# Which weight pairs are summed ahead, when, and a reciprocal on 128x256

## The chip, the cores and the metric

The kernel runs on one core of a Trainium2 chip. The metric is the device time of one execution in microseconds (us), as the median of several runs. The core has a matmul engine (PE; its weight loads are shown apart as PEld), a vector engine (DVE), a scalar engine (ACT), GpSimd (POOL), and SyncE (SP), whose queue issues nearly all transfers (DMAs) between the chip's memory and the on-chip buffers.

## The reference

A decoder trunk of two layers over 512 tokens with 1024 features, in float32. The part of each layer that matters here:

```python
h = rmsnorm(x, g_mix)
z = h @ w_in        # split into attention q, k, v; retention q, k, v, g; two gates
ya = sliding_window_sink_attention(aq, ak, av, sinks) @ w_a
r = chunkwise_retention(rq, rk, rv)
r = r * lax.rsqrt(jnp.mean(r * r, axis=-1, keepdims=True) + EPS)
yb = (r.reshape(B, S, RET_V) * jax.nn.silu(rg)) @ w_b
x = x + (jax.nn.sigmoid(ga) * ya + jax.nn.sigmoid(gb) * yb) @ w_out
h2 = rmsnorm(x, g_mlp)
x = x + jnp.square(jax.nn.relu(h2 @ w_up)) @ w_down
```

`w_in` is 1024 x 5888 here (46 units of 128 columns), `w_b` and `w_out` are 1024 x 1024, `w_up` is 1024 x 4096 and `w_down` 4096 x 1024. A last RMS norm follows the two layers.

## The kernel before

**Layout.** Features lie on the 128 partitions and the 512 tokens in the columns; x is eight chunks of 128x512. Weights are streamed in units of 128x1024 in an order fixed when the program is written (`unit_order`).

**Two parts for each number.** Every operand of a matmul is split into a high part, rounded to the type that PE multiplies fast, and a low part, the rest. A product is three matmuls: high by high, high by low, low by high (`products`, L332 to L334). For a weight unit, ACT copies `hi` (L286) and DVE subtracts to get `lo` (L287). `split_until` does this three units ahead of their use; `hi`, `lo` and the raw weights have three buffers each.

**Pairs.** Most chunks of `w_b` (the first four), `w_out` (the last six) and `w_up` (all but the first four) are computed two at a time by a scheme with seven products in place of eight: x or its counterpart is cut into blocks, sums of these blocks ("forms", `sum_input`, L590 to L594) are multiplied by sums of the two chunks' weights. A pair takes four parts (units), of which the last is half as wide. A narrow pair (`narrow_pair`) multiplies 256 columns at a time with `products`; a wide one (`wide_pair`, chunks 6 to 31 of `w_up`) has its high by high and high by low products in one matmul of 512 columns (L1321), and the low by high in one of 256 (L1322).

**Where the weight sums come from.** Usually DVE makes them in four adds of 128x512 just before the parts are split (`add_part`, L252, L255, L259, L260). Such a pair loads half of its first chunk w1 and its second chunk w2 into two of the three raw buffers, and the other half of w1 into a buffer of the larger pool `big` (seven buffers of 128x1024); part 2 takes one more of these. The sums of the five pairs in `PARKED` are made ahead instead, in every layer: `raws_ahead` loads both chunks into two `big` buffers (L234), `sums_ahead` makes four adds (L241 to L244) and writes the four results to the chip's memory (L246, "parking"), and `load_part` fetches them later (L219): seven loads for the pair in place of three, and no add at that time. Before the change these are the first two pairs of `w_b` and all three of `w_out`.

**Where the sums ahead are placed.** `ahead()` makes the oldest loaded sum and then loads the next pair; two loads precede the first. Its five calls stand, before the change, behind the second head's retention keys and queries (`qk(1)`), behind units 1 and 3 of the retention values (`values`), and behind units 1 and 3 of `w_a`. The last call in `values` stands ahead of the evacuation of the four value banks (`split`, ACT L342 and DVE L343).

**The stages of a layer, in order**, for layer 0: attention's projections, the gates and the first half of the retention projections with attention as a background task that is advanced between matmuls (to about 145 us); the values, and `w_a` (to about 192 us); the rest of `w_in` with retention in the background; `w_b` (about 320 to 360 us); `w_out` (two plain chunks, then three narrow pairs, to about 402 us); the MLP, which begins with a group of four plain chunks of `w_up` in four units, then pairs 4 (narrow) and 6 (wide) back to back, then `w_down` chunks and `w_up` pairs by turns.

**The MLP's norm.** Sums of squares of x come from PE as a matmul with ones, so that every partition holds all tokens' sums (L461). `inverse_rms` takes a root on ACT (L462) and a reciprocal on DVE (L463), both on 128x512; `Rms.finish` calls it behind the second unit of the first group of `w_up`. The four banks of that group are evacuated with it (`put_up`, L1298), and those of pair 4 (`positive`, L1287). The norm ahead of the projections is `folded`: its sums of squares lie on half of the partitions; both norms use the same function.

**Order.** Each engine and SP work strictly in order. That order is made when the program is built: a planner goes through the instructions in the order in which they are written, with estimated durations, and lets a later one go first where an earlier one isn't ready by its estimate. `tc.issue_after(ins)` keeps what stands in it behind `ins`. Buffers are given out by the same planner when their last reader is done.

Of the kernel before, what the change touches and what calls it, by code (L numbers as in the profile page):

```python
# [13 lines left out]
AF = mybir.ActivationFunctionType  # L14
# [4 lines left out]
P = 128  # L19
T = 512  # L20
D = 1024
# [29 lines left out]
ASIDE = 48  # L51
FIRST_WIDE, LAST_WIDE = 6, 32
BETWEEN = (0, 2, 4, 5)
PARKED = (("w_b", 0), ("w_b", 2), ("w_out", 2), ("w_out", 4), ("w_out", 6))
H = T // 2
CROSSED = (0, 1, 4, 5, 2, 3, 6, 7)

# [65 lines left out]
def view(slot):  # L123
    return slot[0][:, slot[1], :]
# [3 lines left out]
def decoder(ctx, tc, xT, x_first, w_in, w_a, w_b, w_out, w_up, w_down, tables, decay, band, triangles, g_last, out):  # L128
    nc = tc.nc
# [8 lines left out]
    ps_aux = ctx.enter_context(tc.tile_pool(name="ps_aux", bufs=3, space=PSUM))  # L138
# [4 lines left out]
    def temp(name="t"):  # L143
        return tmp.tile([P, T], F32, tag="t", name=name)

    def big(name, dtype=F32):
        return tmp.tile([P, 2, T], dtype, tag="big", name=name, bufs=7)

    def bank(pool, name):
        return pool.tile([P, T], F32, tag=pool.name, name=name)  # L150
# [8 lines left out]
    eps, half, keep = (little_x[:, a : a + n] for a, n in ((0, 1), (8, N_KV), (16, P // 2)))  # L159
# [45 lines left out]

    park = {at: dram.tile([P, 4, T], F32, name="park_%s_%d" % at) for at in PARKED}

# [22 lines left out]
    def raws_ahead(layer, src, j):  # L230

        two = [big("ahead").rearrange("p a t -> p (a t)") for _ in range(2)]
        for b, w in enumerate(two):
            nc.sync.dma_start(w, weights[src][layer, j + b])  # L234
        return two
# [56 lines left out]
    def unit(name, layer):  # L292
        i = state["next"]
        assert order[i][:2] == (layer, name), (order[i], layer, name)
        state["next"] += 1
        split_until(i + 3)
        return parts.pop(i)
# [7 lines left out]
    ones = const.tile([P, P], F32R, name="ones")  # L305
# [20 lines left out]
    def products(ps, pairs, start, stop, resume=False):  # L326


        n = len(pairs)
        for i, ((ah, al), (bh, bl)) in enumerate(pairs):  # L330
            more = {"skip_group_check": True} if resume else {}
            nc.tensor.matmul(ps, ah, bh, start=start and i == 0, stop=False, **more)  # L332
            nc.tensor.matmul(ps, ah, bl, start=False, stop=False, **more)  # L333
            nc.tensor.matmul(ps, al, bh, start=False, stop=stop and i == n - 1, **more)  # L334

    def split(hi, lo, src, scale=None):

        if scale is None:
            nc.scalar.activation(hi, src, AF.Copy)  # L339
            nc.vector.tensor_tensor(lo, src, f32(hi), ALU.subtract)  # L340
        else:
            nc.scalar.activation(hi, src, AF.Copy, scale=scale)  # L342
            nc.vector.scalar_tensor_tensor(lo, src, scale, f32(hi), ALU.mult, ALU.subtract)  # L343
# [15 lines left out]
    def advance(rate=1.0):  # L359

        credit[0] += rate
        while credit[0] >= 1.0:
            credit[0] -= 1.0
            while background:
                try:
                    next(background[0])
                    break
                except StopIteration:
                    background.pop(0)

    def drain():
        while background:
            advance()

    def chunk(name, layer, moving, evacuate, rate=1.0):

        hi, lo = unit(name, layer)
        n = len(moving)
        ps = bank(ps_mm, "mm")
        pairs = [((hi[:, k * P : (k + 1) * P], lo[:, k * P : (k + 1) * P]), moving[k]) for k in range(n)]  # L380
        advance(rate)
        products(ps, pairs[: n // 2], True, False)
        advance(rate)
        products(ps, pairs[n // 2 :], False, True)
        evacuate(ps)
# [57 lines left out]
    def inverse_rms_apart(both, n, dest):  # L443
# [10 lines left out]
        nc.sync.dma_start(row, own[0 : P : P // NB, :])  # L454
        nc.sync.dma_start(dest, row.rearrange("b t -> (b t)").unsqueeze(0).broadcast_to([P, T]))

    def inverse_rms(both, n, dest):

        ps = bank(ps_aux, "ssq")
        for i, part in enumerate(both):  # L460
            nc.tensor.matmul(ps, ones, part, start=i == 0, stop=i == len(both) - 1)  # L461
        nc.scalar.activation(dest, ps, AF.Sqrt, bias=eps, scale=1.0 / n)  # L462
        nc.vector.reciprocal(dest, dest)  # L463
# [12 lines left out]
    class Rms:  # L476
# [7 lines left out]

        def finish(self):
            self.value = tmp.tile([P, T], F32, tag="rstd", name="rstd", bufs=2)
            inverse_rms(self.parts, D, self.value)


    def end(layer, uT):  # L490
# [76 lines left out]
    def layer_body(layer):  # L567
# [3 lines left out]
        def rstd():  # L571
            return rms_mix.value
# [78 lines left out]
        def scaled_tables(i):  # L651
            raw, t = big("rawtab"), big("tab")
            nc.sync.dma_start(raw, tables[:, 2 * i : 2 * i + 2, :])
            nc.vector.tensor_tensor(t, raw, rstd().unsqueeze(1).broadcast_to([P, 2, T]), ALU.mult)
            return [t[:, j, :] for j in range(2)]
# [253 lines left out]
        def put_ret(box, h):  # L909
            def put(ps):  # L910
                if not ret_tabs:
                    ret_tabs.extend(scaled_tables(1))
                hi, lo = slots.one(), slots.one()
                split(view(hi), view(lo), rotate(ps, ret_tabs))
                box[h] = (hi, lo)

            return put

        def qk(h, rate=1.0):
            chunk("w_in", layer, xs, put_ret(rk, h), rate)  # L920
            chunk("w_in", layer, xs, put_ret(rq, h), rate)

        rv = {}

        def values(pair, between=lambda: None):

            banks = [bank(ps_mm, "rv") for _ in range(NB)]
            for u in range(4):
                hi, lo = unit("w_in", layer)
                for j in range(2):  # L930
                    k = 2 * u + j
                    cols = slice(j * T, (j + 1) * T)
                    for b, ps in enumerate(banks):
                        at = slice(b * P, (b + 1) * P)
                        products(
                            ps, [(tuple(m[:, at] for m in xs[k]), (hi[:, cols], lo[:, cols]))], k == 0, k == KD - 1
                        )
                    advance()
                if u % 2:
                    between()  # L940
            for b, ps in enumerate(banks):
                hi, lo = slots.one(), slots.one()
                split(view(hi), view(lo), ps, rcol[:, b : b + 1])
                rv[pair, b] = (hi, lo)
# [3 lines left out]
        def put_rg(i):  # L948
            def put(ps):
                if i % 2 == 0:  # L950
                    two = rg_tiles[i // 2] = big("z")
                    rg[i], rg_next[i + 1] = two[:, 0, :], two[:, 1, :]
                else:
                    rg[i] = rg_next.pop(i)
                nc.vector.tensor_tensor(rg[i], ps, rstd(), ALU.mult)
                if i >= 4:
                    silu(i)

            return put

        def silu(i):
            s = temp("sig")
            nc.scalar.activation(s, rg[i], AF.Sigmoid)
            nc.vector.tensor_tensor(rg[i], rg[i], s, ALU.mult)
# [129 lines left out]
        qk(0, PACE)  # L1094
        for i in range(4):
            chunk("w_in", layer, xs, put_rg(i), PACE)
        drain()
        rstd_columns()
        with tc.issue_after(last_exp[0]):
            for hs in (slice(0, T // 2), slice(T // 2, T)):  # L1100
                nc.scalar.activation(x[:, :, hs], x[:, :, hs], AF.Sigmoid)
            for i in range(4):
                silu(i)
        to_load, to_sum = [(layer, *at) for at in PARKED], []

        def load_ahead():
            if to_load:
                to_sum.append((*to_load[0][1:], raws_ahead(*to_load.pop(0))))

        def ahead():  # L1110
            if to_sum:
                with tc.issue_after(last_low[0]):
                    sums_ahead(*to_sum.pop(0))
            load_ahead()

        load_ahead()
        load_ahead()
        qk(1)
        ahead()
        values(0, ahead)  # L1120


        aT = [(a_h[:, c, :], a_l[:, c, :]) for c in range(4)]
        for u in range(4):
            hi, lo = unit("w_a", layer)
            for j in range(2):
                c = 2 * u + j
                ps = bank(ps_mm, "mm")
                pairs = []
                for k in range(4):  # L1130
                    cols = slice(k * 256 + j * P, k * 256 + (j + 1) * P)
                    pairs.append(((hi[:, cols], lo[:, cols]), aT[k]))
                products(ps, pairs, True, True)
                nc.vector.tensor_tensor(mixed[c], mixed[c], ps, ALU.mult)
            if u % 2:
                ahead()
        for t in a_t:
            slots.give(*t[1])
# [2 lines left out]
        qk(2)  # L1141
        qk(3)
        values(1)
        drain()
        background.append(retention(1))
# [301 lines left out]
    for layer in range(DEPTH):  # L1447
        layer_body(layer)
# [175 lines left out]
```

## Time and profile before

| what | value |
|---|---|
| median of three runs | 1478.03 us (1477.93 to 1478.52) |
| the profiled execution's own time | 1478.12 us |
| its span (first to last instruction) | 1476.3 us |
| PE busy | 1465.4 us, 99% |
| PE weight loads busy | 1249.4 us, 85% |
| DVE busy | 1169.0 us, 79% |
| ACT busy | 809.3 us, 55% |
| DMA | 194.45 MB, 132 GB/s on average |

A row of the instructions in order of time reads: start in us from the span's start, length, engine, line, operation, output<-inputs, sizes, count; in brackets the engine's idle time before it and what ended it. A row of the list of waits reads: engine and line, what it waited for, us in total, times, the longest. A group in the profile of one line gives shortest, median and longest duration in ns and the first and last start. In the list of transfers stand line, count, KB each and the median us from issue to landing. Matmuls are pipelined and their ends are modelled, so a busy PE may still lose time between starts.

### The profile page before, as it was taken

Reading aid. Unit: us, or ns where it says so; the run is one execution under the profiler, and the core shown is the slowest. Engines: PE = TensorE matmul, PEld = TensorE weight load, DVE = VectorE, ACT = ScalarE, POOL = GpSimd, SP = SyncE. Lnnn points to the kernel's source line nnn. Section 1 sums busy time; section 2 is a strip of 40 time slices with the busy share of each in tenths; the row PEclk is TensorE's granted clock in tenths of the full one; section 3 lists DMA queues with packets and bytes.
Section 4 is the critical chain, followed back from the end, with each engine's and each line's share of the span. In section 5 each row is a group of like instructions: output and inputs, shape, how many; then the busy total and the mean of one; then the engine's idle time right before and its main releaser. Section 6 shows DMA issues by size and latency. Waiting matters only on the chain.

```text
span 1476.3 us, 20212 instructions
## 1 busy us (share of the span) xinstructions
PE 1465.4 (99%) x7466; PEld 1249.4 (85%) x7466; DVE 1169.0 (79%) x1920; ACT 809.3 (55%) x1296; POOL 3.8 (0%) x14
## 2 busy tenths in 40 slices
PE   9999999999999999999999999999999999999998
PEld 7888788888988888888888888888989888888887
DVE  7998778778898787776678987786888977878763
ACT  6656356654674445444455753656547654444553
POOL 0000000000000000000000000000000000000000
PEclk9999999999999999999999999999999999999999
DMA  6423943356523332333443258333655223333241
GB/s 226 134 88 94 316 134 96 105 170 223 165 79 115 100 111 89 107 107 115 164 124 98 86 167 289 104 103 104 205 180 168 96 93 98 114 101 113 89 140 57
DMA packets 71042, 194.45 MB, mean 132 GB/s; under 512 B 8456, under 2 KB 8608, under 8 KB 70944
## 3 DMA queue, kind: packets, MB, share of 16 engines
q1 hardware_dynamic: 70656, 192.65, 40.6%
q8 instruction: 58, 0.95, 0.3%
q10 hardware_dynamic: 288, 0.52, 0.1%
q14 instruction: 40, 0.33, 0.1%
HBM read 171.63 MB, written 18.89 MB: 129 GB/s over the span
## 4 chain that ended last, share of the span: by engine, by line
PE 90%; issue 5%; DVE 3%; DMA 1%; ACT 1%; POOLq 0%; SPq 0%; DVEq 0%; ACTq 0%
PE mm L334 22%; PE mm L332 22%; PE mm L333 22%; PE mm L1321 10%; PE mm L1322 5%; PE rv L332 2%; PE rv L334 2%; PE rv L333 2%; DVE lo L287 1%; PE score L828 1%; PE r L332 1%; PE r L334 1%; PE r L333 1%; DMA park_w_b<-ahead 0%; PE pT L783 0%
## 5 line engine op out<-in xcount | busy, mean ns | idle before, releaser
L333 PE MATMUL mm<-r,hi 128*128 128x512 f32 (+1 forms) x1568 | 572.8, 367 | 0.0
L332 PE MATMUL mm<-r,hi 128*128 128x512 f32 (+1 forms) x1568 | 570.4, 367 | 1.2 <-DVE r L343 1.2
L334 PE MATMUL mm<-r,lo 128*128 128x512 f32 (+1 forms) x1568 | 564.2, 367 | 0.4
L286 ACT ACTIVATE hi<-raw 128x1024 fp32r<-128x1024 f32 (+1 forms) x334 | 334.1, 1002 | 394.7 <-PE mm L333 193.9
L287 DVE TENSOR_TENSOR lo<-raw,hi 128x512 fp32r<-128x512 f32 (+1 forms) x335 | 384.1, 1150 | 113.1 <-ACT hi L286 109.7
L332 PEld LDWEIGHTS mm<-r,hi 128*128 128x128 f32 x1568 | 294.1, 188 | 48.4 <-DVE r L343 1.5
L334 PEld LDWEIGHTS mm<-r,lo 128*128 128x128 f32 x1568 | 293.7, 188 | 48.9 <-DVE lo L287 1.6
L333 PEld LDWEIGHTS mm<-r,hi 128*128 128x128 f32 x1568 | 294.5, 188 | 45.9
L1321 PE MATMUL mm<-r,hi 128*128 128x512 f32 x728 | 251.9, 391 | 0.0
L1322 PE MATMUL mm<-r,lo 128*128 128x256 f32 x728 | 200.3, 277 | 2.9 <-DVE lo L287 2.7
L1321 PEld LDWEIGHTS mm<-r,hi 128*128 128x128 f32 x728 | 136.4, 188 | 28.3
L1322 PEld LDWEIGHTS mm<-r,lo 128*128 128x128 f32 x728 | 136.7, 188 | 7.0 <-DVE lo L287 4.5
L1401 DVE TENSOR_TENSOR x<-x,mm 128x512 f32<-128x512 f32 x56 | 37.7, 686 | 29.3 <-PE mm L334 29.3
L1394 ACT ACTIVATE z<-z 128x512 f32<-128x512 f32 x56 | 32.5, 624 | 48.3 <-DVE z L1374 48.3
L333 PE MATMUL rv<-lo,r 128*128 128x512 f32 x128 | 49.8, 389 | 0.0
L334 PE MATMUL rv<-hi,r 128*128 128x512 f32 x128 | 49.5, 389 | 0.0
L332 PE MATMUL rv<-hi,r 128*128 128x512 f32 x128 | 49.5, 390 | 0.0
L340 DVE TENSOR_TENSOR r<-z,r 128x512 fp32r<-128x512 f32 x64 | 42.8, 684 | 2.8 <-ACT r L339 2.6
L339 ACT ACTIVATE r<-z 128x512 fp32r<-128x512 f32 x64 | 38.5, 620 | 7.9 <-DVE z L1055 7.9
L855 ACT ACTIVATE sm<-sm,st 128x256 f32<-128x256 f32 (+1 forms) x64 | 30.2, 473 | 19.2 <-DVE st L843 18.9
L1374 DVE SCALAR_TENSOR_TENSOR z<-z,rstd 128x512 f32<-128x512 f32 x52 | 35.7, 686 | 0.6
L343 DVE SCALAR_TENSOR_TENSOR r<-x,r 128x512 fp32r<-128x512 f32 x32 | 23.9, 745 | 7.6 <-ACT r L342 7.5
(267 smaller groups left out, 1696.2 us busy)
## 6 DMA issues: line engine op xcount, KB each, us to landing
raw<-w_in_in SPq DMA_DIRECT2D x89, 512.0 KB, 3.7
raw<-w_down_in SPq DMA_DIRECT2D x64, 512.0 KB, 3.6
raw<-w_up_in SPq DMA_DIRECT2D x36, 512.0 KB, 3.6
raw<-w_up_in SPq DMA_DIRECT2D x56, 256.0 KB, 3.0
ahead<-w_out_in SPq DMA_DIRECT2D x12, 512.0 KB, 5.2
park_w_out<-ahead SPq DMA_DIRECT2D x24, 256.0 KB, 5.2
raw<-park_w_out SPq DMA_DIRECT2D x24, 256.0 KB, 4.3
raw<-w_out_in SPq DMA_DIRECT2D x18, 256.0 KB, 2.8
```

Source lines behind the costliest of these rows:

```text
L286: nc.scalar.activation(hi[:, at], raw[:, at], AF.Copy)
L287: last_low[:] = [nc.vector.tensor_tensor(lo[:, at], raw[:, at], f32(hi[:, at]), ALU.subtract).ins]
L332: nc.tensor.matmul(ps, ah, bh, start=start and i == 0, stop=False, **more)
L333: nc.tensor.matmul(ps, ah, bl, start=False, stop=False, **more)
L334: nc.tensor.matmul(ps, al, bh, start=False, stop=stop and i == n - 1, **more)
L339: nc.scalar.activation(hi, src, AF.Copy)
L340: nc.vector.tensor_tensor(lo, src, f32(hi), ALU.subtract)
L1321: nc.tensor.matmul(both, hi[:, c], m, start=start and k == 0, stop=False, **more)
L1322: nc.tensor.matmul(ps[:, :H], lo[:, c], m[:, 0, :], start=False, stop=k == 3 and start, **more)
L1374: nc.vector.scalar_tensor_tensor(z[:, :, at], z[:, :, at], 0.0, factor, ALU.max, ALU.mult)
L1394: nc.scalar.activation(z[:, i, :], z[:, i, :], AF.Square)
L1401: nc.vector.tensor_tensor(x[:, c, :], x[:, c, :], ps, ALU.add)
```

## The change

- `PARKED` holds five other pairs: the first two of `w_b` as before, the last of `w_out`, and the first two of `w_up` (chunks 4 and 6). The first two pairs of `w_out` are thus summed by `add_part`, and pairs 4 and 6 of `w_up` aren't any more.
- The first two loads ahead stand in front of the drain of the attention task and of what follows it (the retention norm's columns, the sigmoid of the gates and the first SiLUs), no longer behind these.
- The five calls of `ahead()` stand between the second head's keys and queries, behind unit 0 of the values, and behind units 0, 1 and 3 of `w_a`.
- The MLP's norm uses a new function, `inverse_rms_halved`: the root of the first 256 tokens goes to the upper 64 partitions and that of the last 256 to the lower 64, of one 128x256 tile; one reciprocal of 128x256 follows, and four copies on ACT (64x256 each) bring both halves back to all partitions of the 128x512 result. The other norm keeps `inverse_rms`.

```diff
-PARKED = (("w_b", 0), ("w_b", 2), ("w_out", 2), ("w_out", 4), ("w_out", 6))
+PARKED = (("w_b", 0), ("w_b", 2), ("w_out", 6), ("w_up", 4), ("w_up", 6))
...
+    def inverse_rms_halved(both, n, dest):
+
+        ps = bank(ps_aux, "ssq")
+        for i, part in enumerate(both):
+            nc.tensor.matmul(ps, ones, part, start=i == 0, stop=i == len(both) - 1)
+        own = temp("own")[:, : T // 2]
+        sides = [(slice(a * P // 2, (a + 1) * P // 2), slice(a * T // 2, (a + 1) * T // 2)) for a in range(2)]
+        for rows, cols in sides:
+            nc.scalar.activation(own[rows, :], ps[rows, cols], AF.Sqrt, bias=eps[rows, :], scale=1.0 / n)
+        nc.vector.reciprocal(own, own)
+        for rows, cols in sides:
+            for there, _ in sides:
+                nc.scalar.activation(dest[there, cols], own[rows, :], AF.Copy)
...
-            inverse_rms(self.parts, D, self.value)
+            (inverse_rms if self.folded else inverse_rms_halved)(self.parts, D, self.value)
...
-        def qk(h, rate=1.0):
+        def qk(h, rate=1.0, between=lambda: None):
             chunk("w_in", layer, xs, put_ret(rk, h), rate)
+            between()
             chunk("w_in", layer, xs, put_ret(rq, h), rate)
...
-                if u % 2:
+                if u == 0:
                     between()
...
             chunk("w_in", layer, xs, put_rg(i), PACE)
+        to_load, to_sum = [(layer, *at) for at in PARKED], []
+
+        def load_ahead():
+            if to_load:
+                to_sum.append((*to_load[0][1:], raws_ahead(*to_load.pop(0))))
+
+        load_ahead()
+        load_ahead()
         drain()
...
-        load_ahead()
-        load_ahead()
-        qk(1)
-        ahead()
+        qk(1, between=ahead)
         values(0, ahead)
...
-            if u % 2:
+            if u != 2:
                 ahead()
```

More of the change, by code (lines that the diff above doesn't have):

```diff
@@ L1103, in layer_body @@
                 silu(i)
[L1104 to L1108, printed above, removed]
         def ahead():
```

## The prediction

> **What bounds the kernel.** The page comes first: the busy shares and the chain that ended last. Then the waits of the matmul engine PE, its instructions in order of time, the same of the engines it waits for, and the stretches around them.
>
> ```profile
> span 1476.3 us, 20212 instructions
> PE 1465.4 (99%) x7466; PEld 1249.4 (85%) x7466; DVE 1169.0 (79%) x1920; ACT 809.3 (55%) x1296; POOL 3.8 (0%) x14
> PE 90%; issue 5%; DVE 3%; DMA 1%; ACT 1%; POOLq 0%; SPq 0%; DVEq 0%; ACTq 0%
> ...
> PE mm L1322 <- DVE lo L287: 2.7, 2, 1.4
> PE mm L332 <- DVE r L343: 1.2, 1, 1.2
> ```
>
> PE is busy for all but 11 us of the span and carries 90% of the chain. The change removes no matmul, so it can gain only what PE loses between matmuls. The list of waits names three: two of together 2.7 us on `lo` (the low part of a weight unit, L287) and one of 1.2 us on the evacuation of the retention values (L343). A matmul's recorded end lies behind the next one's start, so I measure a loss by the distance of starts, in the instructions in order of time (start, length, engine, line):
>
> ```profile
> 169.44 0.28 PE L334 MATMUL ret<-r 128*128 128x256 f32 x1
> 170.96 0.50 PE L332 MATMUL mm<-r,hi 128*128 128x512 f32 x1 [1.25 <-DVE r L343]
> ...
> 381.52 0.28 PE L333 MATMUL mm<-r,hi 128*128 128x256 f32 x1
> 381.64 0.28 PE L334 MATMUL mm<-r,lo 128*128 128x256 f32 x1
> ...
> 391.41 0.28 PE L333 MATMUL mm<-r,hi 128*128 128x256 f32 x1
> 391.79 0.39 PE L334 MATMUL mm<-r,lo 128*128 128x256 f32 x1
> ...
> 433.68 0.40 PE L1321 MATMUL mm<-r,hi 128*128 128x512 f32 x1
> 435.44 0.39 PE L1322 MATMUL mm<-r,lo 128*128 128x256 f32 x1 [1.36 <-DVE lo L287]
> 435.67 0.40 PE L1321 MATMUL mm<-r,hi 128*128 128x512 f32 x1
> 435.90 0.28 PE L1322 MATMUL mm<-r,lo 128*128 128x256 f32 x1
> ...
> 442.18 0.62 PE L1321 MATMUL mm<-r,hi 128*128 128x512 f32 x2
> 442.91 0.38 PE L1322 MATMUL mm<-r,lo 128*128 128x256 f32 x1
> ...
> 446.04 0.40 PE L333 MATMUL mm<-r,hi 128*128 128x512 f32 x1
> 446.53 0.73 PE L334 MATMUL mm<-r,lo 128*128 128x512 f32 x2
> ...
> 1165.02 0.39 PE L1322 MATMUL mm<-r,lo 128*128 128x256 f32 x1 [1.36 <-DVE lo L287]
> ```
>
> A 256-column matmul is followed after 0.12 us (381.52 to 381.64), a 512-column one after 0.23 (435.67 to 435.90), and the one behind a late one comes 0.1 late too (435.44 to 435.67, where 0.12 is due). So the values' wait costs 170.96 - 169.44 - 0.12 = 1.40, with the next 1.5 us, in layer 0 alone. At the start of the MLP, 435.44 - 433.68 - 0.23 = 1.53; 442.91 comes two 512-column matmuls after 442.18 and 0.27 late; 446.53 is 0.26 late; with 0.1 behind each, 2.4 us in layer 0. The row at 1165.02, with the same idle time on the same releaser, shows it again in layer 1. In the output projection (w_out) a matmul at 391.79 is 0.26 late, with the next 0.4. All that the change aims at is 1.5 + 2 x 2.4 = 6.3 us.
>
> **Why PE waits there.**
>
> ```profile
> 162.10 0.33 SPq L234 DMA_DIRECT2D ahead<-w_out_in  x1
> 168.10 0.69 DVE L241 TENSOR_TENSOR ahead<-ahead 128x512 f32<-128x512 f32 x1 [5.06 <-DMA ahead<-w_out_in]
> 170.17 0.74 DVE L343 SCALAR_TENSOR_TENSOR r<-rv,rcol,r 128x512 fp32r<-128x512 f32 x1
> ...
> 425.89 3.35 DVE L463 RECIPROCAL rstd<-rstd 128x512 f32<-128x512 f32 x1 [0.79 <-ACT rstd L462]
> 429.71 1.81 DVE L287 TENSOR_TENSOR lo<-raw,hi 128x1024 fp32r<-128x1024 f32 x2
> 433.57 0.68 DVE L259 TENSOR_TENSOR raw<-raw 128x512 f32<-128x512 f32 x1
> 434.17 1.22 DVE L287 TENSOR_TENSOR lo<-raw,hi 128x1024 fp32r<-128x1024 f32 x1
> ...
> 371.00:384.00 13.00, 13.00 (x105) 12.64 (x104) 8.76 (x14) 7.36 (x12) 0.00 (x0) 1.00 0.49 142
> 371.00:402.00 31.00, 30.91 (x252) 30.27 (x251) 23.87 (x36) 19.84 (x33) 0.00 (x0) 1.00 0.56 170
> 402.00:447.00 45.00, 43.44 (x247) 37.48 (x246) 44.21 (x61) 35.22 (x51) 0.00 (x0) 1.00 0.30 94
> ```
>
> In layer 0 the third sum (from L241 on) stands on DVE ahead of the values' evacuation (L343). Its load was issued at 162.10, behind the parking of the first sum, so DVE sat 5.06 us waiting for it, and the evacuations came after. At the start of the MLP nothing is late but DVE itself: a reciprocal of 3.35 us, then the adds of the two unparked pairs (the last of them before the wait at 433.57) stand ahead of the `lo` at 434.17, which PE wants behind 433.68. The last three rows are stretches: length, then busy time (and count) of PE, its weight loads, DVE, ACT and POOL, the granted PE clock, the DMA share and GB/s. DVE is full from 402 to 447 (44.2 of 45 us), and has 7.1 us free in the three w_out pairs before it, 4.2 of these before 384. The clock stays at 1.00, so no throttle has to be explained.
>
> **The change part by part.**
>
> *Two pairs of w_up are parked, so the MLP loses adds.* Per pair four adds go (L252, L255, L259, L260); one holds DVE for 0.60 us (433.57 to the next start at 434.17). Eight are 4.8 us per layer; of those behind the reciprocal, three lie ahead of the late `lo`: 1.8 us.
>
> *The reciprocal.*
>
> ```profile
> L452 DVE RECIPROCAL own<-own x6: 952/953/954, 225.3 to 1015.6; 128x128 f32<-128x128 f32 x6
> L451 ACT ACTIVATE own<-ssq,x x24: 358/360/362, 223.8 to 1015.2; 32x128 f32<-32x128 f32 x24
> 425.17 0.69 ACT L462 ACTIVATE rstd<-ssq,x 128x512 f32<-128x512 f32 x1 [1.55 <-PE ssq L461]
> L1327 ACT ACTIVATE side<-mm x52: 362/365/384, 443.9 to 1431.6; 128x256 f32<-128x256 f32 x52
> ```
>
> No row has 256 columns. The 0.95 us at 128 and 3.35 at 512 give 6.25 ns a column, and 0.95 + 128 x 0.00625 = 1.75 us: 1.60 us of DVE are saved per layer. In its place ACT gets a second root and four copies. A root of 256 columns lies between 0.36 (L451, 128 columns) and 0.69 (L462, 512), 0.47 by the same line; a copy of 256 columns took 0.37 (L1327). The path is then 2 x 0.47 + 1.75 + 4 x 0.37 = 4.2 us against 0.69 + 3.35 = 4.0: the norm arrives 0.2 us later, or 0.3 earlier if neighbours on ACT overlap by the 0.1 that the DVE rows show (0.68 long, 0.60 apart). Both ends are small: the gain is DVE's 1.60 us free for `lo`, not an earlier norm. ACT has the room for 1.7 us more: 35.2 of 45 us busy there. If it had not, the copies would hold up the next high part by as much, 1.1 to 1.5 us.
>
> [...]
>
> At 434.17 DVE would thus be 1.8 + 1.6 = 3.4 us ahead of the trace, more than the 1.53 that PE lost, and stays ahead at 442.91. The wait on `lo` goes; what is late next is the raw weight. A parked part takes one of three raw buffers until it is split, so its load starts only when the unit three before it is split. The second part of the second pair must wait for the split at 429.71, whose first half (some 1.1 us) starts 1.6 us earlier behind the shorter reciprocal: 429.2 at its end. Then come
>
> ```profile
> raw<-park_w_out SPq DMA_DIRECT2D x24, 256.0 KB, 4.3
> raw<-w_out_in SPq DMA_DIRECT2D x4, 512.0 KB, 3.6
> DMA to landing us min/median/max: 2.3/5.3/7.3
> 163.00:192.00 29.00, 27.75 (x124) 22.81 (x124) 21.34 (x33) 9.51 (x12) 0.00 (x0) 1.00 0.93 320
> ```
>
> 4.3 us of landing (the parked row), 1.0 of ACT and 1.2 of DVE (1.22 at 434.17; ACT's copy is an estimate, a little under it): 435.7, and PE reaches that part 24 matmuls of 0.12 or their equal, 2.7 us, after 433.68, at 436.4. It fits by 0.7 us, or misses by 0.3 with a landing of 5.3. I keep 0 to 1.0 us of loss per layer and take 0.4, the size of the w_out loss above, the nearest case of one late unit.
>
> *Two pairs of w_out are not parked any more.* Eight adds, 4.8 us, go into the 7.1 us that DVE has free. They fall before about 384, where 4.2 are free, so a little is pushed on into the 2.9 after that: they fit on average, but the cover is thin, and if it is gone they cost up to 4.8 us a layer. The transfers become fewer (three loads a pair for seven). The tight point is the second pair's w2: its buffer comes free when the first pair's last adds have read w1. DVE can do these when it sits free for 1.50 us before 373.02:
>
> ```profile
> 373.02 1.28 DVE L1253 TENSOR_TENSOR x<-x,mm 128x512 f32<-128x512 f32 x2 [1.50 <-PE mm L334]
> ```
>
> The load then goes at 373.2 and lands after 3.6 to 5.3 us (the rows above); add, high and low part (0.7 + 1.0 + 1.2) bring 379.7 to 381.4, and the trace has the first matmul on that low part at 381.64. Cost 0 to 1.0 us a layer, and I take 0.4; a gain of 0.4 is possible, if the loss at 391.79 goes with the heavier parked loads.
>
> *The spread.* The first sum moves ahead of one query chunk, the second ahead by one unit, the third from before the values' evacuations to behind the first unit of w_a; its load landed at 168.10 at the latest, and the evacuations rank first. The 1.5 us go. The sums in w_a add 2.4 us of DVE there, and their loads and stores stand on SP before the next weights; the DMA share from 163 to 192 is 0.93 at 320 GB/s, so a sum may sit waiting for its load again, but then with the other banks and several us of each unit in hand: 0, with 1.5 as the other end. Moving the first two loads ahead of the drain passes no transfer on SP and no buffer request: the 14 chunks before it advance attention by 22 steps (14 x 2 x 0.8), and it has 18.
>
> **Sum.** The profiled run took 1478.12 us: its span and 1.8 us around it, 0.1 above the median. 1478.1 - 6.3 + 2 x 0.4 (MLP) + 2 x 0.4 (w_out) = 1473.4 us.
>
> **Rivals.**
> - *The third sum still stands first.* A planner makes the order on DVE; it may find the sum ready while the evacuations aren't. For it: it mixed the two here (L241 at 168.10, L343 at 170.17). Against: the sum now ranks behind them. 1473.4 + 1.5 = 1474.9.
> - *The queue only moves.* The same 4.8 us of adds arrive just before the full stretch. If they are pushed through 402 instead of into the free slots, the MLP begins later by what it saves, and waits of about 2 us a layer stay in one place or another: 1473.4 + 4 = 1477.4, no change.
> - *The raw buffers* (the other side). Each unparked pair holds two of three raw buffers. If w2 of the second pair has to wait not for the last adds but for the split of the first pair's last part, this row decides:
>
> ```profile
> 376.54 0.69 DVE L287 TENSOR_TENSOR lo<-raw,hi 128x512 fp32r<-128x512 f32 x1 [0.93 <-ACT hi L286]
> ```
>
> It lands at 377.2 + 5.3 and is ready at 385.4: 3.8 us late, and DVE, which works in order, stands before that add with evacuations behind it. Twice 3.8 in place of 0.4 makes 1480.2; with the longest landing of such a load, 7.3, 1484. For: two such pairs in a row. Against: the last adds need no more than the first 1.50 us slot. It decides from 2.8 us a layer on.
>
> **Chances.** Forecast (1471 to 1474.5) 0.48; third sum 0.15; moved queue 0.19; raw buffers 0.18. A measurement tells about 0.2% here, 3 us. Faster by more: the forecast and most of the third-sum case, 0.60. Within: 0.23, the moved queue and the near ends of its neighbours. Slower: 0.17. The low end is all losses gone, those at 391.79 too: 1478.1 - 6.3 - 0.8 = 1471.0. The high end takes in the moved queue and leaves out most of the buffers' case: 1479.
>
> **What would show it.** Right: at about 171 no wait of PE, and L343 ahead of the third sum; no wait on `lo` at the start of either MLP, the reciprocal at 1.75 us, DVE with gaps between 424 and 447; the adds L252 to L260 of w_out between 360 and 385 without a PE wait over 0.5 us. Wrong: DVE sitting on `raw<-w_out_in` between 373 and 385, or ACT on `raw<-park_w_up` between 430 and 436, with PE idle behind it; or a sum that waits for its load with evacuations behind it.

## The result

The median went from 1478.47 us (1477.93 to 1478.61, six runs) to 1472.8 us (1472.3 to 1473.8, six runs): a ratio of 0.9964, with a 95% interval from 0.9953 to 0.9975. The profiled execution took 1473.8 us, its span 1472.0 against 1476.3 before.

The page of the changed kernel: span, busy shares, and the chain that ended last.

```profile
span 1472.0 us, 20220 instructions
...
PE 1464.8 (100%) x7466; PEld 1249.6 (85%) x7466; DVE 1166.7 (79%) x1920; ACT 810.9 (55%) x1306; POOL 3.8 (0%) x14
...
PE 94%; issue 5%; DMA 1%; DVE 0%; ACT 0%; POOLq 0%; DVEq 0%; SPq 0%
```

DVE's part of the chain went from 3% to nothing and PE's from 90% to 94%; the busy times are those of before within 3 us. The list of PE's waits (engine and line, releaser, us in total, times, longest) has none inside a layer any more; both rows lie in the first 7 us of the kernel:

```profile
PE warm L311 <- DVE ones L306: 1.0, 1, 1.0
PE mm L332 <- ACT r L342: 0.6, 1, 0.6
```

PE's instructions in order of time, at the places where it lost time before and where it does now:

```profile
169.56 0.28 PE L332 MATMUL ret<-r 128*128 128x256 f32 x1
...
169.91 0.40 PE L332 MATMUL mm<-r,hi 128*128 128x512 f32 x1
...
380.43 0.28 PE L333 MATMUL mm<-r,hi 128*128 128x256 f32 x1
380.71 0.39 PE L334 MATMUL mm<-r,lo 128*128 128x256 f32 x1
...
432.88 0.40 PE L1336 MATMUL mm<-r,hi 128*128 128x512 f32 x1
433.28 0.39 PE L1337 MATMUL mm<-r,lo 128*128 128x256 f32 x1
433.51 0.40 PE L1336 MATMUL mm<-r,hi 128*128 128x512 f32 x1
```

By distances of starts, as in the prediction: nothing is lost after 169.56 (three matmuls of 256 columns take 0.35, where 0.12 each is due), where 1.5 us went before. At the MLP's start 433.28 comes 0.17 late and the next 0.11: 0.28 us in place of 2.4, and the same 0.28 in layer 1. In w_out the matmul at 380.71 is 0.17 late and its next 0.11; with a like pair at 392.38 w_out loses 0.64 us a layer, 0.3 more than before.

DVE's instructions of the changed kernel show the two places from the other side (start, length, line; the row at 187.72, the first product of the retention, is used further down):

```profile
166.18 2.79 DVE L343 SCALAR_TENSOR_TENSOR r<-rv,rcol,r 128x512 fp32r<-128x512 f32 x4 [2.77 <-ACT r L342]
...
170.31 0.68 DVE L241 TENSOR_TENSOR ahead<-ahead 128x512 f32<-128x512 f32 x1
...
187.72 1.48 DVE L1022 TENSOR_TENSOR s<-ret,dm 128x512 f32<-128x512 f32 x3
...
359.92 0.68 DVE L252 TENSOR_TENSOR raw<-raw 128x512 f32<-128x512 f32 x1
...
366.59 0.68 DVE L259 TENSOR_TENSOR raw<-raw 128x512 f32<-128x512 f32 x1
367.20 0.68 DVE L260 TENSOR_TENSOR raw<-raw 128x512 f32<-128x512 f32 x1
...
372.41 0.68 DVE L252 TENSOR_TENSOR raw<-raw 128x512 f32<-128x512 f32 x1
...
379.10 0.42 DVE L656 TENSOR_TENSOR z<-mm,eu 128x256 f32<-128x256 f32 x1 [0.33 <-PE mm L334]
379.44 1.22 DVE L287 TENSOR_TENSOR lo<-raw,hi 128x1024 fp32r<-128x1024 f32 x1
...
425.13 1.75 DVE L466 RECIPROCAL own<-own 128x256 f32<-128x256 f32 x1 [3.14 <-ACT own L465]
426.80 1.16 DVE L287 TENSOR_TENSOR lo<-raw,hi 128x1024 fp32r<-128x1024 f32 x1
428.65 0.69 DVE L1313 SCALAR_TENSOR_TENSOR up<-mm,rstd 128x512 f32<-128x512 f32 x1 [0.69 <-ACT rstd L469]
...
432.01 1.22 DVE L287 TENSOR_TENSOR lo<-raw,hi 128x1024 fp32r<-128x1024 f32 x1
```

The four evacuations of the values stand at 166.18, ahead of the third sum at 170.31, where the sum had been first. The adds of the two unparked w_out pairs run from 359.92 on. The reciprocal takes 1.75 us. The idle times in brackets at 425.13 and 428.65 say that DVE now waits for work there; the stretches say the same (length, busy time and count of PE, weight loads, DVE, ACT, POOL, clock, DMA share, GB/s):

```profile
355.00:371.00 16.00, 16.00 (x74) 13.33 (x73) 15.96 (x23) 7.17 (x9) 0.00 (x0) 1.00 0.54 164
371.00:402.00 31.00, 30.91 (x249) 29.99 (x248) 27.88 (x43) 20.98 (x34) 0.00 (x0) 1.00 0.36 112
402.00:447.00 45.00, 45.00 (x257) 39.25 (x256) 40.34 (x57) 35.63 (x55) 0.00 (x0) 1.00 0.46 141
163.00:192.00 29.00, 29.00 (x132) 24.09 (x131) 21.80 (x33) 9.17 (x12) 0.00 (x0) 1.00 0.93 331
```

DVE's work fell by 3.9 us in 402-447 (44.2 to 40.3 of 45) and grew by 4.0 in 371-402 (23.9 to 27.9 of 31). Before that it stayed full; the row of the kernel before is

```profile
355.00:371.00 16.00, 16.00 (x72) 13.26 (x71) 15.78 (x21) 7.39 (x9) 0.00 (x0) 1.00 0.53 163
```

so the first pair's four adds (359.92 to 367.20) pushed other work behind 371, and the second pair's four came on top.

ACT around the norm, in order of time:

```profile
420.56 1.28 ACT L465 ACT_TABLE_LOAD   x1
424.15 0.95 ACT L465 ACTIVATE own<-ssq,x 64x256 f32<-64x256 f32 x2 [2.31 <-PE ssq L461]
425.12 1.06 ACT L286 ACTIVATE hi<-raw 128x1024 fp32r<-128x1024 f32 x1
...
426.92 1.70 ACT L469 ACTIVATE rstd<-own 64x256 f32<-64x256 f32 x4 [0.34 <-DVE own L466]
...
430.91 1.04 ACT L286 ACTIVATE hi<-raw 128x1024 fp32r<-128x1024 f32 x1
```

From the start of the roots (424.15) to the end of the copies (426.92 + 1.70) the norm takes 4.47 us, against 4.07 before (425.17 to 425.89 + 3.35): 0.4 us longer, not shorter. From 426.92 on ACT has no idle time before 434.1 us, and the high part at 430.91 is one of the instructions that stand behind the copies.

### The profile page after: what moved, and what is told of

Read it like the earlier page. It is cut to its first block, busy times and chain, and to the rows that moved or that the text cites. A ratio compares the mean times of both kernels' runs of the same rounds, so it can differ in the third digit from the quotient of the medians.

```text
span 1472.0 us, 20220 instructions
## 1 busy us (share of the span) xinstructions
PE 1464.8 (100%) x7466; PEld 1249.6 (85%) x7466; DVE 1166.7 (79%) x1920; ACT 810.9 (55%) x1306; POOL 3.8 (0%) x14
## 4 chain that ended last, share of the span: by engine, by line
PE 94%; issue 5%; DMA 1%; DVE 0%; ACT 0%; POOLq 0%; DVEq 0%; SPq 0%
PE mm L334 22%; PE mm L332 22%; PE mm L333 22%; PE mm L1336 11%; PE mm L1337 5%; PE rv L332 2%; PE rv L333 2%; PE rv L334 2%; PE score L842 1%; PE r L332 1%; PE r L334 1%; PE r L333 1%; PE pT L797 0%; PE pv L823 0%; PE pv L824 0%
## 5 line engine op out<-in xcount | busy, mean ns | idle before, releaser
L340 DVE TENSOR_TENSOR r<-sums,r 128x1024 fp32r<-128x1024 f32 x24 | 28.9, 1220 | 0.0
```

## The experiments

Each kernel was timed in five rounds beside the kernel before on the same chip. The last column is worked out from the starts of PE's instructions as in the prediction (losses over 0.1 us, the one behind a late matmul included). The profiled runs of e1 to e10 lie within 0.5 us of their medians.

| run | median us | ratio to before, 95% | PE's losses, us a layer (layer 0 and 1 where they differ) |
|---|---|---|---|
| the change | 1472.80 | 0.9964 [0.9953, 0.9975] | values 0, w_out 0.64, MLP 0.28 |
| e1 full reciprocal | 1473.76 | 0.9970 [0.9958, 0.9981] | MLP 0.7 |
| e2 old pairs | 1474.64 | 0.9975 [0.9966, 0.9985] | w_out 0.4, MLP 1.4 |
| e3 old places | 1474.90 | 0.9975 [0.9965, 0.9985] | values 1.5 (once), MLP 0.28 |
| e4 w_out's middle pair parked | 1478.67 | 1.0004 [0.9996, 1.0013] | w_out 3.3 and 3.6, MLP 0.28 |
| e5 e4, w2 elsewhere | 1479.03 | 1.0006 [0.9997, 1.0015] | w_out 0.9, MLP 3.2 |
| e6 change, w2 elsewhere | 1480.21 | 1.0014 [1.0005, 1.0022] | w_out 1.3, MLP 3.3 |
| e7 sixth pair | 1485.78 | 1.0052 [1.0039, 1.0064] | w_b 4.5 and 2.6, w_out 0.65, MLP 3.2 |
| e8 other five pairs | 1483.05 | 1.0036 [1.0023, 1.0048] | w_b 2.1 and 1.5, w_out 0.7, MLP 3.3 |
| e9 e5, one copy later | 1474.58 | 0.9972 [0.9962, 0.9982] | w_out 0.65, MLP 1.3 and 0.7 |
| e10 e7, one copy later | 1481.55 | 1.0021 [1.0012, 1.0030] | w_b 3.8 (5.3 with the slower clock, see below) and 2.5, w_out 0.65, MLP 0.9 and 0.7, 0.5 once near 200 us |

**One part undone at a time (e1, e2, e3).**

```diff
 # e1: the full reciprocal in Rms.finish
-            (inverse_rms if self.folded else inverse_rms_halved)(self.parts, D, self.value)
+            inverse_rms(self.parts, D, self.value)
 # e2: the pairs of before
-PARKED = (("w_b", 0), ("w_b", 2), ("w_out", 6), ("w_up", 4), ("w_up", 6))
+PARKED = (("w_b", 0), ("w_b", 2), ("w_out", 2), ("w_out", 4), ("w_out", 6))
 # e3: loads and calls of ahead() where they stood before; PARKED and the norm as changed
```

> The change without the short reciprocal (the MLP's norm is the full one, 128x512, as before). Theory (DVE's lead decides at the start of the MLP): the parked pairs alone put DVE 1.8 us ahead of the late low part, more than the 1.53 us lost there, and 2.4 us ahead at the next loss of 0.27; so the waits there stay nearly gone, PE loses under 0.8 us a layer there, and the time is within 1 us of the changed kernel, about 1473.5. Rival (both parts are needed): the lead without the reciprocal is eaten by the later copies of raw weights, 1 to 2 us a layer come back, 1475 to 1477.

> The change with the five pairs of before (all of w_out parked, none of w_up), summed at the new places, and with the short reciprocal. Theory (lead of DVE): the reciprocal alone gives 1.6 us of lead against a loss of 1.53, barely enough for the first wait, and the third sum's wait in layer 0 is gone: -1.5 - 2 x (1.5 to 2.4), 1471.8 to 1473.6. Rival (the adds are what holds DVE there): at most a part of the first wait goes, 1474.5 to 1476.6.

> The change with the sums ahead at the places of before. Theory: the third sum stands ahead of the values' evacuation again and waits for its load; PE waits 1.2 to 1.5 us on L343 at about 171 in layer 0, and the start of the MLP is as in the changed kernel: changed kernel + 1.5, about 1474.3. Rival (the wait went because of another pair's load, or the order by the planner is a matter of chance): no wait there, 1472.8; or waits at another place too, over 1475.5.

PE's waits of e2 and of e3 (the row that each has and the change has not):

```profile
PE mm L1337 <- DVE lo L287: 1.1, 2, 0.5
```

```profile
PE mm L332 <- DVE r L343: 1.2, 1, 1.2
```

e3 brings the values' wait back, 1.2 us as before the change, and nothing at the MLP: the spread is worth 1.5 us of PE, and 2.1 us in the medians. What does it is the places of the sums, as far as the queue shows: the loads that the edit writes earlier are not issued earlier (the first at 144.78 us, against 144.40 before; the second load of the third sum at 163.46, against 162.10). e3 moves loads and sums back together, so no run separates the two. e2, whose time fits the rival and not the theory, brings the wait on `lo` back at a third of its size (1.1 us in two layers for 2.7): the reciprocal alone takes 1.0 us a layer off the 2.4, and the parking of the w_up pairs added to it the other 1.1. In e1 the wait of 1.53 is gone without the short reciprocal; 0.7 us a layer stay in small pieces, 0.4 more than in the change: the parking alone takes 1.7. That is 0.9 us in two layers, and the times don't resolve it: the intervals of e1 and the change overlap, and e1's profiled span is 1471.9, as short as the change's, since e1 loses 0.6 us less at the kernel's start. The intervals of e2 and e3 overlap the change's too; what ties the parts to the gain are PE's rows, not the times alone.

**Which w_out pair stays parked (e4), and the buffer (e5, e6).**

```diff
 # e4
-PARKED = (("w_b", 0), ("w_b", 2), ("w_out", 6), ("w_up", 4), ("w_up", 6))
+PARKED = (("w_b", 0), ("w_b", 2), ("w_out", 4), ("w_up", 4), ("w_up", 6))
 # e5: e4, and in load_part the second chunk w2 of w_out's last pair goes into the larger pool
-            raws[i + 3] = raw_tile()
+            raws[i + 3] = big("raw4").rearrange("p a t -> p (a t)") if (src, j) == ("w_out", 6) else raw_tile()
 # e6: the change, and the same for both unparked pairs of w_out
```

> The changed kernel with the fourth and fifth chunks of w_out parked in place of the last two, so that the two unparked pairs of w_out (chunks 2 and 6) don't follow each other. Theory of the raw buffers: the two losses of 0.28 and 0.36 us a layer in w_out come from two unparked pairs back to back; apart, both pairs find their buffers free and the 0.6 us a layer shrink to 0.3 or less, -0.7 us in all. Rival (DVE's and ACT's queues are the cause): the losses stay at 0.5 to 0.8 us a layer, or grow, since the adds of the last pair now fall next to the full stretch at 402: 0 to +2 us.

> The kernel of the run before (chunks 4 and 5 of w_out parked, the last two not), but w2 of the last w_out pair is loaded into one of the seven large buffers instead of one of the three raw ones. Theory (the raw buffer is what made w2 late: its load went at 385.1, at a buffer's release, and its add at 388.75 came just behind the landing): the load goes several us earlier, the two losses of 1.06 and 2.0 us a layer shrink to 0.7 together or less, 1478.7 - 2 x 2.4 = 1473.9. Rival (DVE's adds next to the full stretch are too many): the load is early and the losses stay above 2 us a layer, 1477 or more.

> The changed kernel with w2 of both unparked w_out pairs in large buffers. Theory: in the changed kernel the raw buffers were free in time (its second w2 went at 367.3 and was added at 372.4), and the 0.28 and 0.36 us a layer lost in w_out come from work ahead of the high and low parts on ACT and DVE; so nothing changes, 1472.8 within 0.7. Rival (a late w2 there too): w_out's losses fall by half, -0.7 us.

e4 was to show that two unparked pairs back to back are the risk; it showed the reverse, 5.9 us in the medians, more than the rival had allowed too. PE's waits of e4, then its SP queue, its DVE and its ACT in order of time:

```profile
PE mm L334 <- DVE lo L287: 3.5, 2, 1.7
PE mm L332 <- ACT hi L286: 1.8, 2, 1.0
```

```profile
385.14 0.33 SPq L225 DMA_DIRECT2D raw<-w_out_in  x1
```

```profile
383.88 1.23 DVE L287 TENSOR_TENSOR lo<-raw,hi 128x1024 fp32r<-128x1024 f32 x1 [0.27 <-ACT hi L286]
...
388.75 0.69 DVE L252 TENSOR_TENSOR raw<-raw 128x512 f32<-128x512 f32 x1
```

```profile
389.62 2.01 ACT L286 ACTIVATE hi<-raw 128x1024 fp32r<-128x1024 f32 x2 [1.61 <-DVE raw L252]
393.29 1.06 ACT L286 ACTIVATE hi<-raw 128x1024 fp32r<-128x1024 f32 x1 [1.67 <-DVE raw L260]
```

The load of w2 (L225) goes out at 385.14, as soon as a low part of the parked pair has been read out of its raw buffer (383.88 + 1.23); the first add (L252) starts at 388.75 only, and ACT waits 1.61 us for it. In the changed kernel the second unparked pair has its load out at 367.34, when the first pair's third add (366.59 + 0.68, L259, the last that reads w1) releases w1:

```profile
367.34 0.33 SPq L225 DMA_DIRECT2D raw<-w_out_in  x1
```

A parked pair holds each raw buffer until its own split; an unparked one lets w1 go at its adds, 9 us before its last low part is made (376.11 in the change). So the bad neighbour of an unparked pair is a parked one ahead of it. In e5 that load has a buffer of its own, goes out 8.8 us earlier, and the wait is gone:

```profile
376.35 0.42 SPq L225 DMA_DIRECT2D raw<-w_out_in  x1
```

w_out's loss falls from 3.3 and 3.6 to 0.9 us a layer, so the raw buffer is shown as the cause. The time, expected at 1473.9, stays where it was: 3.2 us a layer turn up at the start of the MLP, which the edit doesn't touch. e6 was expected to change nothing and took 7.4 us longer: with the buffers apart w_out loses more (1.3), and the MLP loses 3.3, so it shifted the order elsewhere and says little on w2. That w2 isn't what the changed kernel waits for in w_out is read from its own row: the add at 372.41 starts with no idle time on a load ahead of it. What is late at 380.71 and 392.38 in the change is a `lo` on DVE with other work ahead of it: at 379.10 an evacuation, although the `hi` for 379.44 is done on ACT at 379.17; from 389.50 to 391.10 an evacuation, a split of x and a sum of squares, although the `hi` is done at 389.66.

**A sixth pair (e7), and other five (e8).**

```diff
 # e7: six pairs, and a call of ahead() behind every unit of w_a
-PARKED = (("w_b", 0), ("w_b", 2), ("w_out", 6), ("w_up", 4), ("w_up", 6))
+PARKED = (("w_b", 0), ("w_b", 2), ("w_out", 4), ("w_out", 6), ("w_up", 4), ("w_up", 6))
...
-            if u != 2:
-                ahead()
+            ahead()
 # e8
-PARKED = (("w_b", 0), ("w_b", 2), ("w_out", 6), ("w_up", 4), ("w_up", 6))
+PARKED = (("w_b", 0), ("w_out", 4), ("w_out", 6), ("w_up", 4), ("w_up", 6))
```

> The changed kernel with a sixth pair parked (chunks 4 and 5 of w_out) and a sixth call behind unit 2 of w_a; one pair of w_out is left unparked. Theory (adds in w_out cost 0.3 us a layer): w_out's losses go back from 0.64 to about 0.4 us a layer, and the sums' stage takes the four adds in DVE's free time: 1472.3. Rival (the transfers are full in the sums' stage, 0.93 of the DMA engines' time from 163 to 192): another 4 MB there in two layers make weights or sums late, with new waits of 1 us or more between 160 and 210: 1474 or more.

> The changed kernel with the second w_b pair unparked and chunks 4 and 5 of w_out parked in its place: w_b's first pair, w_out's last two, w_up's first two. Theory (what counts is where DVE is short and whether w2 finds a raw buffer): the w_b pair's adds fall at about 325 to 335, behind a parked pair, as in the run with the parked pairs apart, so its w2 comes late: 1 to 3 us a layer lost there, 1475 to 1478. Rival (DVE alone decides; it has free time there): no loss in w_b, and 0.25 us less a layer in w_out: 1472.3.

In e7 the stretch of the sums and DVE inside it:

```profile
163.00:192.00 29.00, 29.00 (x131) 24.01 (x130) 21.18 (x30) 7.93 (x9) 0.00 (x0) 1.00 0.99 335
```

```profile
185.75 0.69 DVE L241 TENSOR_TENSOR ahead<-ahead 128x512 f32<-128x512 f32 x1 [3.97 <-DMA ahead<-w_up_in]
...
194.33 0.69 DVE L241 TENSOR_TENSOR ahead<-ahead 128x512 f32<-128x512 f32 x1 [1.89 <-DMA ahead<-w_up_in]
194.94 1.48 DVE L1022 TENSOR_TENSOR s<-ret,dm 128x512 f32<-128x512 f32 x3
```

The transfers are full there (0.99, against 0.93) and DVE sits 3.97 and 1.89 us on a load; yet PE loses nothing between 160 and 215. The losses come later, in w_b (the largest 1.79 us at 335.42) and at the MLP, so neither expectation had the place. The trace shows a path from the one to the other. The sixth sum waits for its load with the retention's first product behind it, which starts at 194.94 where the change has it at 187.72. The retention, a background task, stays that late: the last root of its norm stands at 307.53 on ACT, 301.06 in the change. Until then PE has projections to do in the meantime. In w_b the rest of the retention and the gates fill DVE (16.0 of 16 us from 310 to 326, 12.3 in the change), the splits and loads of w_b's parked parts come after them, and ACT sits idle for 6.14 us until 334.04 on one of these loads. e5, e6 and e8, which have five sums, have that root between 300.3 and 300.8. No edit tests this path.

In e8 an unparked w_b pair follows a parked one, and its first add waits for its load as in e4:

```profile
327.39 0.69 DVE L252 TENSOR_TENSOR raw<-raw 128x512 f32<-128x512 f32 x1 [2.21 <-DMA raw<-w_b_in]
```

That load goes out at 321.88, just behind a low part of the parked pair (320.27 + 1.23). The loss in w_b is as expected (1 to 3 us a layer); the time is 5 us above the range that went with it, since the MLP loses 3.3 a layer as well. Here no run gives the load a buffer of its own.

**The loss at the MLP's start (e9, e10).** e5 to e8 have one row in common, with the same numbers in each; ACT in order of time (of e5) stands behind it:

```profile
PE mm L332 <- ACT own L465: 3.2, 2, 1.6
```

```profile
423.54 1.06 ACT L286 ACTIVATE hi<-raw 128x1024 fp32r<-128x1024 f32 x1 [3.66 <-issue]
424.62 1.28 ACT L465 ACT_TABLE_LOAD   x1
425.92 0.95 ACT L465 ACTIVATE own<-ssq,x 64x256 f32<-64x256 f32 x2
```

A high part stands ahead of the table load and the roots here; in the changed kernel the table load lies in an idle stretch at 420.56 and the same high part behind the roots at 425.12. The next pair needs the bank of PSUM (the buffer that matmuls write) that the roots read. One edit tests it: in e9 and e10 that one split is kept behind the roots: its high part, its low part and the load issued with it.

```diff
 # unit(); e9: e5 with this, e10: e7 with this (state["root"]: the second root of inverse_rms_halved)
-        split_until(i + 3)
+        with tc.issue_after(state["root"]) if name == "pair" and order[i - 1][1] == "w_up" != order[i][1] else nullcontext():
+            split_until(i + 3)
```

> This is the kernel of e5 (w_out's chunk 4 parked, w2 of its last pair in a larger buffer) with one instruction moved at the start of each MLP: the high part copied on ACT at 423.54 us, ahead of the table load and the roots of the norm, is kept behind the roots. In e5 PE loses 1.76 us at 426.92, waiting for the roots (1.6 in each layer by its waits), and 0.24 and 0.79 later, 2.8 us a layer. Theory A, the order on ACT makes that loss: the roots come 1.1 us earlier and the table load falls into ACT's idle stretch ahead of them, the wait on the roots goes in both layers, the losses fall to the 0.3 us a layer of the changed kernel, and the time from 1479.0 to between 1473.5 and 1475.5 us. Theory B, the order only chooses who is late: the high part comes about 2.5 us later, its low part with it, and PE loses 1 to 2 us there in place of the roots: 1477 to 1480 us, with a wait on the low part (L287) behind 427 us.

> This is the kernel of e7 (a sixth pair parked) with the same high part kept behind the roots. e7 took 1485.8 us, 2.8 us a layer of its losses at the start of the MLP and the rest in w_b and w_out, whose cause is open. Theory A, the loss at the MLP is of the same making as in e5: 2 x 2.5 us go, 1480 to 1481.5 us, and the losses in w_b stay where they are. Theory B, a sixth pair makes the MLP late in another way (its loads and stores): the time stays at 1485 to 1487 us.

Waits of PE in e9, and its ACT:

```profile
PE mm L332 <- ACT hi L286: 0.4, 1, 0.4
```

```profile
419.71 1.28 ACT L465 ACT_TABLE_LOAD   x1
423.53 0.95 ACT L465 ACTIVATE own<-ssq,x 64x256 f32<-64x256 f32 x2 [2.54 <-PE ssq L461]
424.51 1.06 ACT L286 ACTIVATE hi<-raw 128x1024 fp32r<-128x1024 f32 x1
```

The wait on the roots is gone in both kernels and 4.45 and 4.23 us of time with it (1479.03 to 1474.58, 1485.78 to 1481.55). Theory A holds for the wait on the roots: the order on ACT makes it (or that of the load and the low part, which the edit moves too). That it is the bank that PE waits for is read from the names, not tested apart. e9 is no better than the change: its MLP loses 1.3 and 0.7 us, not the 0.3 expected, on high and low parts from 436.79 on, so a part of the loss did move, as theory B has it. In e10 the losses in w_b stay (the largest 1.65 at 335.18), and the retention's root is as late as in e7 (307.44). In e10's profiled execution PE's granted clock was also 0.57 on average from 337 to 341 (0.998 over the whole execution), with 256-column matmuls 0.21 us apart in place of 0.12; this costs 1.5 us more there, and none of the other profiled executions shows such a stretch inside a layer. No kernel here beats the change.

## Why the prediction came out as it did

- *Where PE lost time, and how much*: right. The values, w_out and the MLP's start are the only places inside a layer where PE's losses changed by 0.1 us or more. Of 6.3 us, 1.5 went at the values, as predicted, and at the MLP 2 x 2.1 of 2 x 2.4.
- *What the MLP keeps*: taken as 0.4 a layer, measured 0.28. It was put down to a late raw part; it is a `lo` (432.01 to 433.23) whose `hi` ends on ACT only at 431.95 (430.91 + 1.04), with no wait on a transfer. The prediction gave ACT the room for the copies on average (35.2 of 45 us busy) and named the other case: copies that hold up the next high part. That case is the nearer one. In the change this high part starts 6.76 us behind the start of the root, in e1, which has no copies, 5.98 us (429.48 behind 423.50), and there PE loses nothing at that matmul. That 0.28 lies near 0.4 is luck.
- *What the unparked w_out pairs cost*: taken as 0.4 a layer, measured 0.28 (0.64 for 0.36). Its working failed in one step. It had the first pair's last adds in DVE's free slot before 373, so w2 loaded at 373.2 and in time by 0.2 to 1.9 us. They ran at 366.59 and 367.20, in a stretch where DVE is full, and w2 was loaded at 367.34, 6 us earlier: they stand ahead of other work, which went behind 371 in their place. I had looked for free slots, and what counts is the order. The room between 371 and 402 did take it, 4.0 of 7.1 us, and what is late there is a `lo` behind other work on DVE, not a weight. Here too a size near the 0.4 came from another mechanism than the one that was priced.
- *The reciprocal*: 1.75 us by the line through 128 and 512 columns, measured 1.75; the root 0.47, measured 0.47 (0.95 for two). The four copies were put at 0.37 each, 1.5; they took 1.70, 0.42 each and 0.43 apart, so neighbours on ACT didn't overlap as the low end of the range had it. The row of 0.37 (`side<-mm`) is of other copies: 128x256 from `mm`, where these are 64x256 from `own`; which difference makes the 0.05 us no run shows. The norm came 0.4 us later after its roots began, outside the range of 0.2 later to 0.3 earlier: 0.2 us of it are the longer copies, 0.07 the two hand-overs between ACT and DVE (425.10 to 425.13, 426.88 to 426.92). Two roots of 64x256 took 0.95 us, one of 128x512 took 0.69: a root of half the columns on half the partitions is 0.22 us shorter (0.47 for 0.69), not half.
- *DVE's lead at 434.17 of 3.4 us*: two independent sources for one wait of 1.53. e1 and e2 show that parking alone would have removed that wait, and the reciprocal alone not: it left 0.71 at 433.26. The 1.6 us of the reciprocal did not all reach the `lo`.
- *The third sum still first, and the moved queue* didn't happen: the evacuations stand at 166.18, and the adds lie ahead of 402. That moving the first two loads changes nothing was right as well (144.78 against 144.40).
- *The raw buffers*: the mechanism is there, near the size worked out (3.8 us a layer; w_out loses 3.3 and 3.6 in e4, 0.3 of it at the other pair), but the condition was wrong. Two unparked pairs in a row found their buffers free here; an unparked one behind a parked one didn't (shown by e4 with e5; e8 has the same row).
- *The sum*: with the measured terms 1478.1 - 1.5 - 2 x 2.1 + 2 x 0.3 + 0.4 = 1473.4. The 0.4 is a longer wait for the first transfers of the kernel (1.14 us lost against 0.75), which was no term of mine and changes from run to run. The profiled 1473.8 is 0.4 above that: losses under 60 ns each, which I didn't follow up. The medians stand 5.7 us apart and the profiled executions 4.3, since the profiled execution of the change is the slowest of its six; the traces explain the 4.3, and the other 1.4 us is not accounted for.

## What to carry to other kernels

Measure a full engine's losses by the distance of its starts, not by its busy share: PE showed 99% before and 100% after, and all that the change gained were gaps of 0.3 to 1.5 us at two places. Work that is moved to a fuller or emptier stretch should be followed to the buffers that it holds and to the moment it lets each go, since the same adds cost 0.3 us a layer behind one neighbour and about 3 behind another. A background task that starts late may cost nothing where it starts, and show up where the work that covers it ends (in layer 0 of e7 PE lost nothing between 160 and 215 us and 4.5 us in w_b; no edit tests the path between them). Where a planner makes the order, an edit can shift an instruction elsewhere: look at each engine's order in the stages that weren't touched before a difference in time is put down to the edit.

## What was not expected of the hardware

- A reciprocal took 0.95 us at 128 columns, 1.75 at 256 and 3.35 at 512: a straight line, 6.25 ns a column, where the add of 128x512 took 0.68 us in all.
- With the transfers 0.99 busy at 335 GB/s over 29 us (e7), PE lost nothing in that stretch. The 4.5 us that it lost some 130 us later lie at the end of the path by way of the retention's late start, which the trace shows and no edit tests.
- The table load ahead of the roots takes 1.28 us. In an idle stretch of ACT (420.56 in the change, 419.71 in e9) PE has no wait on the roots; behind a 1.06 us copy in e5 to e8 it is part of a wait of 1.6 us in each layer.
